# Sample rows' value and output projections as fp32 products in four column tiles, and VectorE left out of the branch around the exact path

## The chip, the cores and the metric

The kernel runs on one core of a Trainium2 chip. The metric is the device time of one execution in microseconds (us). Three runs of the kernel before took 1475.44, 1479.99 and 1482.45 us, median 1479.99. One more execution was profiled: 1477.82 us, of which the span from the first to the last instruction is 1476.1 us, with a mean granted TensorE clock of 0.99. Engines go by their short names in the profile's lines: PE is TensorE's products (PEld its weight loads), DVE is VectorE, ACT ScalarE, POOL GpSimd, SP SyncE, which issues all DMAs here. A q behind the name (DVEq) is an engine's sequencer.

## What is computed

One layer of a streaming encoder in fp32, for 1024 new rows of a prompt and 32 next rows of a running stream (the sample rows), with a model width of 1024:

```python
u = rmsnorm(x, pre_norm_g) @ w_in           # split into gq, gk, gv, gr, gg, dq, dk, dv, dg, ma, mb
...
o_gla, state = gla(gq, gk, gv, log_a)       # chunked gated linear attention with a decay
o_diff = diff_attend(rope(dq), rope(dk), dv, mask, lam)
...
yg = rmsnorm(o_gla, gla_norm_g) * silu(gg)
yd = rmsnorm(o_diff, diff_subln_g) * (1.0 - lambda_init) * silu(dg)
merged = sigmoid(ma) * (yg @ w_proj_gla) + sigmoid(mb) * (yd @ w_proj_diff)
y = x + rmsnorm(merged @ w_out, post_norm_g)
```

Three pieces matter here: the value projections (gv and dv, 1024 columns each), the last projection `merged @ w_out`, and inside the linear attention the matrix of a chunk, which weighs query t and key s by the exponential of a difference of summed decays.

## The kernel before, in words

**Products in two parts.** A matrix is split into a high part in fp32r and the rest (the low part, also fp32r), and a product becomes three: high by high, low by high, high by low. `X` holds the high and low parts of the normalized input (1024 prompt rows, then 32 sample rows), `wh` and `wl` those of weights; ScalarE makes the high part from the raw weights `wr`, VectorE or GpSimd subtracts it for the low part.

**Stages, in order.** (1) Norm and value projections, 0 to 220 us: for u = 0 to 3 a piece of 512 columns of gv and dv. A row tile has 128 rows, NQ = 8 tiles for the prompt; for each, 24 products of 512 columns run into one of two PSUM banks (`value_mm`, L295 to 308), ScalarE copies the bank to `vo`, SP stores it (`value_tile`, L283 to 293). (2) The GLA stage, 220 to about 510 us, and the attention stage after it, both with projections in between. (3) The two output branches, then `merged @ w_out` from 1372 us to the end: for u = 0 to 3 a piece of 256 columns of w_out, for each the 8 row tiles and then the sample rows (L1207 to 1238).

**The sample rows.** They fill a quarter of a row tile. In stages 1 and 3 they are the ninth tile of each u (i = NQ). `sample_pair` (L254) copies the high and low parts of the 32 rows side by side, 64 columns, into one tile `xsm` (of X) or `mgs` (of the merged rows `mg`); both use the tag "pair" with one buffer. `sample_mm` (L261) makes 16 products of it: 8 of the 64 columns with wh and 8 of the 32 high columns with wl. The result lies in PSUM rows 0 to 31 and 32 to 63; ScalarE copies one half (L291, L1223) and VectorE adds the other (L292, L1224).

**The order of the work.** In u = 0 (and for the work ahead of u = 1) the order on PE, ACT, DVE and POOL is the order of the source (`manual_schedule`). For u = 1 to 3 and in the last stage a scheduler orders each engine's queue when the kernel is built, by the source's order and by what is ready. In the GLA and attention stages PE's order alone is written by hand, by a planner (`Order`) with costs and due times; the other queues are the scheduler's. An engine takes its queue strictly in order.

**Weights of the value stage.** `wr` has one buffer, `wh` and `wl` have two; the weights of u + 1 are loaded and split while u runs. In the last stage the raw w_out pieces go through one buffer with the tag "cwr" (L1187), and the split weights of all four u stay in SBUF.

**The branch.** The fast form of a GLA head's chunk matrix (`ar`) divides the decays into two factors; where the summed decay b falls under a limit, `gla_exact` (L596) makes `ar` in an exact way instead, level by level. `gla_prep` sets a flag `fl` of one number (L554); `gla_exact` has every engine load it (L599, TENSOR_LOAD) and branch around the body (L600, COMPARE_BRANCH). With these inputs no head needs the body. In the body VectorE reads b, q and k and writes `ar`, the temporaries `t1` and `t2` among others. After it follow, per head, ScalarE's split of `ar` (L636), VectorE's in-place change of b (L643), the decayed keys k (L646) and PE's transposes of them (L654); the gated outputs go through PE's transposes L740 and VectorE's L743. L456 is GpSimd's low part of the next projection's weights.

Of the kernel before, what the change touches and what calls it, by code (L numbers as in the profile page):

```python
# [11 lines left out]
F32 = mybir.dt.float32  # L12
# [8 lines left out]
P = 128  # L21
NP = 1024
# [104 lines left out]
def hybrid_step_kernel(ctx: ExitStack, tc: tile.TileContext, a):  # L127
# [133 lines left out]
    def sample_mm(ps, pair, wh, wl):  # L261
# [4 lines left out]
        for k in range(1, KT):  # L266
            mm(ps[0:64], pair[:, k, :], wh[:, k, :], start=False, stop=(k == KT - 1))


    def value_weights(u):  # L270
        wr = v1.tile([P, KT, 512], F32, tag="wr", name="wr")
        wh = v1.tile([P, KT, 512], F32R, tag="wh", bufs=2, name="wh")
        wl = v1.tile([P, KT, 512], F32R, tag="wl", bufs=2, name="wl")
        for k in range(0, KT, 2):
            k2 = slice(k, k + 2)
            dma(wr[:, k2], a["wv"][u, :, k2])
            yield wh, wl
            act(wh[:, k2], wr[:, k2], AF.Copy)
            yield wh, wl
            ve.tensor_tensor(wl[:, k2], wr[:, k2], wh[:, k2].bitcast(F32), op=ALU.subtract)  # L280
            yield wh, wl

    def value_tile(u, i, ps):  # L283
        t0 = i * P
        dst = (gvd if u < 2 else a["newv"])[:, (u % 2) * 512 : (u % 2) * 512 + 512]
        vo = v1.tile([P, 512], F32, tag="vo", bufs=2, name="vo")
        if i < NQ:
            act(vo, ps, AF.Copy)  # L288
            st(dst[t0 : t0 + P, :], vo)
        else:  # L290
            act(vo[0:32], ps[32:64], AF.Copy)  # L291
            ve.tensor_tensor(vo[0:32], ps[0:32], vo[0:32], op=ALU.add)  # L292
            st(dst[NP:T, :], vo[0:32])

    def value_mm(i, wh, wl, meanwhile=lambda: None):  # L295
# [54 lines left out]
    with tc.manual_schedule(engines={E.PE, E.Activation, E.DVE, E.Pool}):  # L350

        def warm(n):
            ps = obank("ps_warm")
            for _ in range(n):
                mm(ps[:, 0:P], one_h, one_h, start=True, stop=True)
        warm(10)
        norm_square(0)
        s = norm_scale(0)
        warm(9)
        w0 = value_weights(0)  # L360

# [60 lines left out]
        act(le, ls, AF.Exp)  # L422
        neglam = cst.tile([P, 1], F32, name="neglam")
        ve.tensor_tensor(neglam, le[:, 1:2], le[:, 0:1], op=ALU.subtract)
        ve.tensor_scalar(neglam, neglam, LAM_INIT, None, op0=ALU.subtract)
        coef = cst.tile([P, 1], F32, name="coef")
        ve.memset(coef, 1.0)
        for r in (32, 96):
            ve.tensor_copy(coef[r : r + 32], neglam[r : r + 32])
        wv = nxt  # L430
    for u in range(1, 4):
        nxt = list(value_weights(u + 1))[-1] if u < 3 else None
        for i in range(NQ + 1):
            value_tile(u, i, value_mm(i, *wv))
        wv = nxt
        if u == 1:
            gate_rank(wgs)
# [157 lines left out]

    def gla_exact(h):  # L596

        q, k, b, qh, ql, ar, fl = gst8[h]
        flag = nc.values_load(fl[0:1, 0:1], min_val=0, max_val=1)  # L599
        with tc.If(flag > 0):  # L600
            for li, half in enumerate(LEVELS + [0]):
                mask = gp.tile([P, P], F32, tag="sm", name="mask")
                dma(mask, a["masks"][li])
                if half:
                    blk = 2 * half
                    ncol = T if blk <= NS else NP
                    e1 = gp.tile([P, T], F32, tag="t1", name="e1")
                    e2 = gp.tile([P, T], F32, tag="t2", name="e2")
                    bv = b[:, :ncol].rearrange("p (c s) -> p c s", s=blk)
                    ref = bv[:, :, half - 1 : half].to_broadcast([P, ncol // blk, blk])  # L610
                    for dst, i0, i1, src in ((e1, bv, ref, q), (e2, ref, bv, k)):
                        dv = dst[:, :ncol].rearrange("p (c s) -> p c s", s=blk)
# [3 lines left out]
                        ve.tensor_tensor(dst[:, :ncol], dst[:, :ncol], src[:, :ncol], op=ALU.mult)  # L616
                else:
                    e1, e2, ncol = q, k, T
                for c in range(9 if ncol == T else 8):
                    w = P if c < 8 else NS  # L620
                    ps = tbank("ps_e")
                    mm(ps[0:w, 0:w], e2[:, c * P : c * P + w], e1[:, c * P : c * P + w], start=True, stop=True)
                    if li == 0 or (c == 8 and half == NS // 2):
                        ve.tensor_tensor(ar[0:w, c, 0:w], ps[0:w, 0:w], mask[0:w, 0:w], op=ALU.mult)
                    else:
                        tm = gp.tile([P, P], F32, tag="sqj", name="tm")
                        ve.tensor_tensor(tm[0:w, 0:w], ps[0:w, 0:w], mask[0:w, 0:w], op=ALU.mult)
                        ve.tensor_tensor(ar[0:w, c, 0:w], ar[0:w, c, 0:w], tm[0:w, 0:w], op=ALU.add)

    def gla_head(h):  # L630
        q, k, b, qh, ql, ar, fl = gst8[h]
# [575 lines left out]
    for u in range(4):  # L1207
        wh, wl = cw[u]
        csl = slice(u * 256, u * 256 + 256)
        for i in range(NQ + 1):  # L1210
            t0 = i * P
            w = P if i < NQ else NS
            ps = (bank, dbank)[i % 2]("ps_c")[:, 0:256]
            if i < NQ:
                for k in range(KT):
                    mm(ps, mg[k][:, 0, t0 : t0 + P], wh[:, k, :], start=(k == 0), stop=False)  # L1216
                    mm(ps, mg[k][:, 1, t0 : t0 + P], wh[:, k, :], start=False, stop=False)  # L1217
                    mm(ps, mg[k][:, 0, t0 : t0 + P], wl[:, k, :], start=False, stop=(k == KT - 1))  # L1218
                src = ps
            else:  # L1220
                sample_mm(ps, mgs, wh, wl)
                tl = op.tile([NS, 256], F32, tag="tl", name="tl")
                act(tl, ps[32:64], AF.Copy)  # L1223
                ve.tensor_tensor(tl, ps[0:32], tl, op=ALU.add)  # L1224
                src = tl
            sqj = op.tile([P, 256], F32, tag="sqj", name="sqj")
            act(sqj[0:w], src[0:w], AF.Square, accum_out=ssq[0:w, i, u : u + 1])
# [97 lines left out]
```

## Time and profile before

| | before |
|---|---|
| median of the runs shown (range) | 1479.99 us (1475.44 to 1482.45) |
| profiled execution | 1477.82 us |
| its span | 1476.1 us |
| DVE busy | 789.9 us, 54% |
| ACT busy | 600.5 us, 41% |
| POOL busy | 300.2 us, 20% |
| moved by DMA | 156.58 MB |

In the lines of a timeline the columns are the start in us from the span's start, the busy time in us, engine, line, operation, out<-in by the program's names, shape and count; in brackets stands how long the engine was idle just before and what ended that. Rows that follow each other with the same form are merged (x8). A product's time contains the depth of PE's pipeline, so products overlap in these rows, and the distance of two starts is what one costs.

### The profile page before, as it was taken

Reading aid. Unit: us, or ns where it says so; the run is one execution under the profiler, and the core shown is the slowest. Engines: PE = TensorE matmul, PEld = TensorE weight load, DVE = VectorE, ACT = ScalarE, POOL = GpSimd, SP = SyncE. Lnnn points to the kernel's source line nnn. Section 1 sums busy time; section 2 is a strip of 40 time slices with the busy share of each in tenths; the row PEclk is TensorE's granted clock in tenths of the full one; section 3 lists DMA queues with packets and bytes.
Section 4 is the critical chain, followed back from the end, with each engine's and each line's share of the span. In section 5 each row is a group of like instructions: output and inputs, shape, how many; then the busy total and the mean of one; then the engine's idle time right before and its main releaser. Section 6 shows DMA issues by size and latency. Waiting matters only on the chain.

```text
span 1476.1 us, 22367 instructions
## 1 busy us (share of the span) xinstructions
PE 1422.4 (96%) x8848; PEld 1327.5 (90%) x8848; DVE 789.9 (54%) x1464; ACT 600.5 (41%) x1262; POOL 300.2 (20%) x186
## 2 busy tenths in 40 slices
PE   8999999989999999899999999999899899999997
PEld 6787779889999899899989998998899799999997
DVE  5602005756565343576776766678665536455415
ACT  4513114535354233455555555555455432221311
POOL 1200002222223124223222222222221111122001
PEclk9999999999999999999999999999999999999999
DMA  8620111122222233313232332223222278634205
GB/s 303 211 107 31 45 50 50 54 73 73 87 64 86 71 109 110 98 54 116 68 100 69 97 90 93 75 77 90 92 69 80 96 265 306 222 132 132 101 1 193
DMA packets 66742, 156.58 MB, mean 106 GB/s; under 512 B 10008, under 2 KB 28568, under 8 KB 65600
## 3 DMA queue, kind: packets, MB, share of 16 engines
q1 hardware_dynamic: 66624, 155.01, 32.5%
q8 instruction: 74, 1.21, 0.4%
q14 instruction: 44, 0.36, 0.1%
HBM read 104.39 MB, written 40.04 MB: 98 GB/s over the span
## 4 chain that ended last, share of the span: by engine, by line
PE 51%; DVE 6%; DMA 4%; ACT 2%; issue 1%; POOL 1%; SPq 0%; DVEq 0%; POOLq 0%; ACTq 0%
PE ps_w L486 9%; PE ps_w L487 9%; PE ps_w L488 9%; PE ps_w L465 2%; PE ps_w L464 2%; PE ps_w L466 2%; PE ps_s L907 2%; PE ps_t L954 2%; PE ps_s L906 2%; PE ps_c L1216 2%; PE ps_c L1218 2%; PE ps_c L1217 2%; DMA ydr<-ydd 1%; DMA kl<-kl 1%; PE po L968 1%
## 5 line engine op out<-in xcount | busy, mean ns | idle before, releaser
L486 PE MATMUL ps_w<-X,wh 128*128 128x352 f32 x1344 | 452.5, 337 | 1.4 <-DVE vo L292 1.1
L487 PE MATMUL ps_w<-X,wl 128*128 128x352 f32 x1344 | 437.7, 326 | 0.0
L488 PE MATMUL ps_w<-X,wh 128*128 128x352 f32 x1344 | 435.7, 324 | 0.0
L456 POOL TENSOR_TENSOR wl<-wr,wh 128x1024 fp32r<-128x1024 f32 x72 | 180.5, 2507 | 656.3 <-ACT wh L454 493.1
L486 PEld LDWEIGHTS ps_w<-X,wh 128*128 128x128 f32 x1344 | 255.0, 190 | 5.5 <-issue 3.0
L487 PEld LDWEIGHTS ps_w<-X,wl 128*128 128x128 f32 x1344 | 255.4, 190 | 1.2 <-issue 1.2
L488 PEld LDWEIGHTS ps_w<-X,wh 128*128 128x128 f32 x1344 | 254.7, 190 | 0.0
L912 ACT ACTIVATE p<-ps_s,nm 128x256 f32<-128x256 f32 (+7 forms) x128 | 94.6, 741 | 58.8 <-DVE ps_s L908 30.8
L306 PE MATMUL ps_v<-wh,X 128*128 128x512 f32 x248 | 97.6, 394 | 1.2 <-DVE X L245 1.2
L305 PE MATMUL ps_v<-wh,X 128*128 128x512 f32 x248 | 98.5, 397 | 0.2 <-DVE g L343 0.2
L307 PE MATMUL ps_v<-wl,X 128*128 128x512 f32 x248 | 98.3, 396 | 0.0
L454 ACT ACTIVATE wh<-wr 128x1024 fp32r<-128x1024 f32 x72 | 75.9, 1054 | 54.6 <-PE ps_w L488 30.6
L910 DVE TENSOR_REDUCE nm<-ps_s 128x1 f32<-128x256 f32 (+7 forms) x128 | 94.8, 747 | 2.7
L292 DVE TENSOR_TENSOR vo<-ps_v,vo 32x512 f32<-32x512 f32 x4 | 2.7, 678 | 140.8 <-ACT vo L291 140.8
L908 DVE MEMSET ps_s<- 64x64 f32 x128 | 14.3, 112 | 115.9 <-PE ps_s L907 114.3
L671 POOL TENSOR_TENSOR vl<-vr,vh 128x512 fp32r<-128x512 f32 (+1 forms) x20 | 24.6, 1228 | 219.4 <-ACT vh L670 219.4
L906 PE MATMUL ps_s<-k,q 128*128 128x512 f32 (+2 forms) x192 | 68.0, 362 | 1.2 <-DMA k<-k 1.2
L907 PE MATMUL ps_s<-kl,q 128*128 128x512 f32 (+2 forms) x192 | 63.8, 348 | 3.7 <-DMA kl<-kl 3.7
L288 ACT ACTIVATE vo<-ps_v 128x512 f32<-128x512 f32 x32 | 19.1, 595 | 115.1 <-PE ps_v L307 114.7
L956 ACT ACTIVATE ah<-ps_t 128x512 fp32r<-128x512 f32 (+2 forms) x96 | 46.9, 488 | 43.5 <-PE ps_t L954 42.7
L957 DVE TENSOR_TENSOR al<-ps_t,ah 128x512 fp32r<-128x512 f32 (+2 forms) x96 | 53.2, 554 | 18.3 <-ACT ah L956 17.0
L465 PE MATMUL ps_w<-Y,wl 128*128 128x352 f32 x192 | 62.2, 324 | 0.0
(319 smaller groups left out, 2968.8 us busy)
## 6 DMA issues: line engine op xcount, KB each, us to landing
wr<-w SPq DMA_DIRECT2D x72, 512.0 KB
thd<-gate SPq DMA_DIRECT2D x16, 528.0 KB
xn<-xn SPq DMA_DIRECT2D x16, 512.0 KB
wr<-wv SPq DMA_DIRECT2D x16, 512.0 KB
newk<-rr SPq DMA_DIRECT2D x8, 528.0 KB
ygr<-ygd SPq DMA_DIRECT2D x8, 528.0 KB
tha<-thd SPq DMA_DIRECT2D x8, 528.0 KB
ydr<-ydd SPq DMA_DIRECT2D x8, 528.0 KB
```

Source lines behind the costliest of these rows:

```text
L305: mm(ps, xk[:, 0, t0 : t0 + P], wh[:, k, :], start=(k == 0), stop=False)
L306: mm(ps, xk[:, 1, t0 : t0 + P], wh[:, k, :], start=False, stop=False)
L307: mm(ps, xk[:, 0, t0 : t0 + P], wl[:, k, :], start=False, stop=(k == KT - 1))
L456: nc.gpsimd.tensor_tensor(wl, wr, wh.bitcast(F32), op=ALU.subtract)
L465: mm(ps[:, :n], wl[:, k, :], src[k][:, 0, t0 : t0 + n], start=False, stop=False)
L486: mm(ps[:, :n], wh[:, k, :], src[k][:, 0, t0 : t0 + n], start=(k == 0), stop=False)
L487: mm(ps[:, :n], wl[:, k, :], src[k][:, 0, t0 : t0 + n], start=False, stop=False)
L488: mm(ps[:, :n], wh[:, k, :], src[k][:, 1, t0 : t0 + n], start=False, stop=(k == KT - 1))
L906: mm(ps[:, n0 : n0 + n], qs[m][:, qsl], ks[m][:, n0 : n0 + n], start=True, stop=False)
L907: mm(ps[:, n0 : n0 + n], qs[m][:, qsl], kls[m][:, n0 : n0 + n], start=False, stop=True)
L910: ve.tensor_reduce(nm, ps[:, 0:w], axis=AX.X, op=ALU.max, negate=True)
L912: act(p[:, 0:w], ps[:, 0:w], AF.Exp, bias=nm, accum_out=sm[:, m : m + 1])
```

## The change

It replaces the sample rows' products for u = 1 to 3 of the value stage and for all u of the last stage; u = 0 of the value stage keeps `sample_pair` and `sample_mm`. `sample_whole` adds high and low part of the 32 rows on GpSimd to one fp32 tile (tag "pair"; `xsw`, `mgs`). `sample_tiled` makes 8 products of fp32 operands, the rows' 32 columns by the raw weights, each in one of four column tiles of PE (column 0, 32, 64 or 96) with its own 32 PSUM rows; `sample_sum` adds the four parts with one ScalarE copy and three VectorE adds. In the value stage the sample tile moves from the end of u to its beginning, and reads `wr`. In the last stage each u loads its raw piece of w_out again, into the buffer "cwr".

In `gla_exact` the flag is loaded by PE, ACT, POOL and SP and no longer by VectorE. The body's VectorE work moves to GpSimd; ScalarE first copies the products out of PSUM, in groups of up to four chunks in a bank, to a tile `tm` with a tag of its own.

```diff
+    def sample_whole(src, name):
+        t = cst.tile([P, 2, KT, NS], F32, tag="pair", name=name)[:, 0]
+        for k in range(KT):
+            nc.gpsimd.tensor_tensor(t[:, k], *(src[k][:, n, NP:T].bitcast(F32) for n in range(2)), op=ALU.add)
+        return t
+
+    def sample_tiled(ps, x, w):
+        for k in range(KT):
+            r = k % 4 * NS
+            mm(ps[r : r + NS], x[:, k, :], w[:, k, :], start=k < 4, stop=k >= 4, tile_position=(0, r))
+
+    def sample_sum(dst, ps):
+        act(dst, ps[32:64], AF.Copy)
+        for r in (0, 64, 96):
+            ve.tensor_tensor(dst, ps[r : r + NS], dst, op=ALU.add)
...
+            if u:
+                sample_sum(vo[0:32], ps)
+            else:
+                act(vo[0:32], ps[32:64], AF.Copy)
+                ve.tensor_tensor(vo[0:32], ps[0:32], vo[0:32], op=ALU.add)
...
         value_tile(0, NQ, ps)
+        xsw = sample_whole(xs, "xsw")
         wgs = gate_weights()
...
     for u in range(1, 4):
+        ps = bank("ps_v")
+        sample_tiled(ps, xsw, wrs[u])
+        value_tile(u, NQ, ps)
         nxt = list(value_weights(u + 1))[-1] if u < 3 else None
-        for i in range(NQ + 1):
+        for i in range(NQ):
             value_tile(u, i, value_mm(i, *wv))
...
-        flag = nc.values_load(fl[0:1, 0:1], min_val=0, max_val=1)
+        en = mybir.EngineType
+        pv = nc.gpsimd
+        flag = nc.values_load(fl[0:1, 0:1], engines=[en.PE, en.Activation, en.Pool, en.SP], min_val=0, max_val=1)
         with tc.If(flag > 0):
...
-                        ve.tensor_tensor(dv, i0, i1, op=ALU.subtract)
-                        ve.tensor_scalar(dst[:, :ncol], dst[:, :ncol], 0.0, None, op0=ALU.min)
+                        pv.tensor_tensor(dv, i0, i1, op=ALU.subtract)
+                        pv.tensor_scalar(dst[:, :ncol], dst[:, :ncol], 0.0, None, op0=ALU.min)
...
+                    act(tm, ps.rearrange("p (c s) -> p c s", s=P)[0:w, 0:n, 0:w], AF.Copy)
...
+                        pv.tensor_tensor(to, tm, mb, op=ALU.mult)
...
-    mgs = sample_pair(mg, "mgs")
+    mgs = sample_whole(mg, "mgs")
...
     for u in range(4):
         wh, wl = cw[u]
         csl = slice(u * 256, u * 256 + 256)
+        raw = cp.tile([P, KT, 256], F32, tag="cwr", name="raw")
+        dma(raw, a["wout"][u])
...
-                sample_mm(ps, mgs, wh, wl)
+                sample_tiled(ps, mgs, raw)
                 tl = op.tile([NS, 256], F32, tag="tl", name="tl")
-                act(tl, ps[32:64], AF.Copy)
-                ve.tensor_tensor(tl, ps[0:32], tl, op=ALU.add)
+                sample_sum(tl, ps)
```

More of the change, by code (lines that the diff above doesn't have):

```diff
@@ L267, in sample_mm @@
             mm(ps[0:64], pair[:, k, :], wh[:, k, :], start=False, stop=(k == KT - 1))
+    def sample_whole(src, name):
[11 more added lines that the diff above has]
+            ve.tensor_tensor(dst, ps[r : r + NS], dst, op=ALU.add)
+    wrs = {}
     def value_weights(u):
-        wr = v1.tile([P, KT, 512], F32, tag="wr", name="wr")
+        wr = wrs[u] = v1.tile([P, KT, 512], F32, tag="wr", name="wr")
         wh = v1.tile([P, KT, 512], F32R, tag="wh", bufs=2, name="wh")
@@ L617, in gla_exact @@
                 else:
                     e1, e2, ncol = q, k, T
-                for c in range(9 if ncol == T else 8):
-                    w = P if c < 8 else NS
+                for c0 in (0, 4, 8)[: 3 if ncol == T else 2]:
+                    n, w = (4, P) if c0 < 8 else (1, NS)
                     ps = tbank("ps_e")
-                    mm(ps[0:w, 0:w], e2[:, c * P : c * P + w], e1[:, c * P : c * P + w], start=True, stop=True)
-                    if li == 0 or (c == 8 and half == NS // 2):
-                        ve.tensor_tensor(ar[0:w, c, 0:w], ps[0:w, 0:w], mask[0:w, 0:w], op=ALU.mult)
-                    else:
-                        tm = gp.tile([P, P], F32, tag="sqj", name="tm")
-                        ve.tensor_tensor(tm[0:w, 0:w], ps[0:w, 0:w], mask[0:w, 0:w], op=ALU.mult)
-                        ve.tensor_tensor(ar[0:w, c, 0:w], ar[0:w, c, 0:w], tm[0:w, 0:w], op=ALU.add)
+                    for c in range(c0, c0 + n):
+                        o = slice((c - c0) * P, (c - c0) * P + w)
+                        mm(ps[0:w, o], e2[:, c * P : c * P + w], e1[:, c * P : c * P + w], start=True, stop=True)
+                    tm = gp.tile([P, 4, P], F32, tag="tm", name="tm")[0:w, 0:n, 0:w]
+                    act(tm, ps.rearrange("p (c s) -> p c s", s=P)[0:w, 0:n, 0:w], AF.Copy)
+                    to = ar[0:w, c0 : c0 + n, 0:w]
+                    mb = mask[0:w, 0:w].unsqueeze(1).to_broadcast([w, n, w])
+                    if li == 0 or (c0 == 8 and half == NS // 2):
+                        pv.tensor_tensor(to, tm, mb, op=ALU.mult)
+                    else:
+                        pv.tensor_tensor(tm, tm, mb, op=ALU.mult)
+                        pv.tensor_tensor(to, to, tm, op=ALU.add)
```

4 lines of the change are left out of this document (1 added, 3 removed).

## The prediction

> **What bounds the kernel now.** I read the page first (busy times, waits, the chain that ended last), then the timeline of each place that the change touches, engine by engine.
>
> ```profile
> span 1476.1 us, 22367 instructions
> PE 1422.4 (96%) x8848; PEld 1327.5 (90%) x8848; DVE 789.9 (54%) x1464; ACT 600.5 (41%) x1262; POOL 300.2 (20%) x186
> ```
>
> PE is busy in 96% of the span and takes its instructions in order, so the end moves by two things only: PE time that goes away, and PE waits that grow or shrink. VectorE is busy for half the time; what it saves counts only where PE waits behind it. The profiled execution took 1477.82 us, 1.7 us more than its span and 2.2 us under the median of the runs shown (1479.99); I sum against 1477.82 and shift the result by 2.2 us.
>
> **Term 1, the value tiles of the sample rows (u = 1 to 3).** One such tile now, in the timeline of PE:
>
> ```profile
> 64.36 0.39 PE L263 MATMUL ps_v<-wh,xsm 128*64 128x512 f32 x1
> 64.59 2.01 PE L265 MATMUL ps_v<-wl,xsm 128*32 128x512 f32 x8
> 66.44 1.77 PE L267 MATMUL ps_v<-wh,xsm 128*64 128x512 f32 x7
> 68.05 0.40 PE L305 MATMUL ps_v<-wh,X 128*128 128x512 f32 x1
> ```
>
> Durations contain the pipeline; starts tell the cost. 1 + 8 + 7 = 16 products take PE from 64.36 to 68.05: 3.69 us, 0.23 us each. The new form has 8 products of fp32 operands, 32 columns wide, in the four column tiles 0, 32, 64 and 96. The trace has such work: the sample rows' attention scores, four fp32 products of 512 columns, in the tiles (row 0, column 0), (64, 32), (0, 64), (64, 96).
>
> ```profile
> 730.02 0.32 PE L488 MATMUL ps_w<-X,wh 128*128 128x352 f32 x1
> ...
> 730.26 0.65 PE L1009 MATMUL ps_ss<-kc,smp 64*32 64x512 f32 x4
> ...
> 730.72 0.63 PE L1009 MATMUL ps_ss<-kc,smp 64*32 64x512 f32 x4
> ...
> 731.15 0.26 PE L1011 MATMUL ps_ss<-smp 64*32 64x32 f32 x8
> 731.34 0.43 PE L486 MATMUL ps_w<-X,wh 128*128 128x352 f32 x1
> ```
>
> Eight records for four products: an fp32 product runs as two passes. All four first passes start together at 730.26 and the second ones at 730.72; the next work follows at 731.15. So a pass of 512 columns takes 0.43 to 0.46 us, whether one tile is at work or four. In the new form each tile has two products, four passes: 0.46 + 3 x 0.43 = 1.75 us. Going in and out costs some 0.3 us: L488 starts at 730.02 and would be followed at 730.18 (352 columns pass in 0.16 us) but is followed at 730.26; after the last short pass comes some 0.1 us of emptying, and the first product behind it is 0.1 us longer (0.43 against 0.32). That makes 2.05 us, and 1.64 us saved per tile, **4.9 us** for three.
>
> Here the trace leaves a gap: its four tiles share each row half by twos, while in the change all four use all 128 rows. Two products that share rows and differ in column (column tiles 0 and 64) do overlap in these rows, and overlap in full; that is the nearest row and I take it. The other end is products one after the other, as where all passes are in one tile:
>
> ```profile
> 748.16 1.06 PE L1041 MATMUL po_s<-vcs,smp 128*32 128x128 f32 x8
> ```
>
> Eight passes of 128 columns in about 1 us, 0.12 us each, none overlapping. Serial passes of 512 columns would make 16 x 0.43 + 0.3 = 7.2 us a tile, 3.5 us worse than now.
>
> A rule speaks against the change. The Trainium skill, TensorE: Matmul & The Clock Gate, Part 3 (what overlaps and what doesn't) says that a weight load overlaps products in flight only when its row group differs. By it the four tiles, all on one row group, would queue, and the result would be the serial rival below. The rows above disagree with it as far as they reach: tiles sharing a row half started their passes together.
>
> **Term 2, the output tiles of the sample rows.** The same for 256 columns:
>
> ```profile
> 1394.40 0.28 PE L263 MATMUL ps_c<-cwh,mgs 128*64 128x256 f32 x1
> 1394.52 1.07 PE L265 MATMUL ps_c<-cwl,mgs 128*32 128x256 f32 x8
> 1396.25 0.28 PE L1216 MATMUL ps_c<-C,m 128*128 128x256 f32 x1
> ```
>
> 1.85 us now; four passes of half the length and 0.3 us make 1.16 us: 0.7 us saved. The tile of u = 3 is the last and has a term of its own; the other three give **2.1 us**.
>
> **Term 3, the tail.** VectorE, not PE, sets the end:
>
> ```profile
> 1468.46 1.42 DVE L1236 SCALAR_TENSOR_TENSOR ogwwl<-ogwwl,s,xn 128x512 f32<-128x512 f32 x2 [0.73 <-POOL s L182]
> 1469.79 0.40 DVE L1224 TENSOR_TENSOR tl<-ps_c,tl 32x256 f32<-32x256 f32 x1
> ```
>
> The add of the last sample tile waits in VectorE's order behind the two L1236 of tile 7. An earlier PE doesn't help it, and sample_sum makes three adds of one: 2 x 0.40 = **0.8 us lost**. Elsewhere the two more adds lie beside the next tile's 24 products, 24 x 0.11 = 2.7 us (output) or 24 x 0.23 = 5.5 us (value).
>
> **Term 4, the hand-over to the GLA stage.** The sample tile now comes ahead of the eight others, so the last bank is emptied by ScalarE alone.
>
> ```profile
> 217.34 0.60 ACT L288 ACTIVATE vo<-ps_v 128x512 f32<-128x512 f32 x1 [5.00 <-PE ps_v L307]
> ...
> 221.02 0.59 ACT L291 ACTIVATE vo<-ps_v 32x512 f32<-32x512 f32 x1 [3.09 <-PE ps_v L267]
> 221.64 0.68 DVE L292 TENSOR_TENSOR vo<-ps_v,vo 32x512 f32<-32x512 f32 x1 [47.80 <-ACT vo L291]
> 222.38 0.43 PE L486 MATMUL ps_w<-X,wh 128*128 128x352 f32 x1 [1.12 <-DVE vo L292]
> ```
>
> The copy takes 0.6 us either way and the add of 0.68 us goes: of PE's wait of 1.12 us **0.7 us go**; the copy is late next.
>
> **Term 5, new waits.** xsw takes the one buffer that xsm has, so GpSimd may write it only after the products of u = 0 have read xsm, and PE's next tile wants it at once. Nearest row for the adds:
>
> ```profile
> 62.19 1.49 POOL L258 CAST xsm<-X 128x64 fp32r<-128x64 f32 x8 [3.21 <-DVE X L245]
> ```
>
> 0.19 us each: the first is there about 0.5 us after PE's 68.05, the last four are needed later than they come, and the fourth tile starts about 1 us late: at most 1.0 us. The other end is zero, if products of tile 0 stand first. The memsets of gate_weights behind the adds on GpSimd slip 5 to 7 us and ScalarE's a2s copies with them; both have the 5.5 us of a tile and more before anyone waits.
>
> The value weights are kept until the next tile read them, so wr of u + 1 loads at the start of u instead of earlier: a whole u (8 x 5.5 + 2 = 46 us) before its use, free. The raw copy of w_out is not free. It takes the buffer of the staged weights, after the last conversion:
>
> ```profile
> 1384.89 0.33 SPq L1188 DMA_DIRECT2D cwr<-wout  x1
> ...
> 1381.06 0.39 ACT L1227 ACTIVATE sqj<-ps_c 128x256 f32<-128x256 f32 x1 [2.25 <-PE ps_c L1218]
> 1381.70 2.19 ACT L1196 ACTIVATE C<-cwr 128x512 fp32r<-128x512 f32 x4 [0.17 <-DMA cwr<-wout]
> ...
> 1389.75 2.19 ACT L1196 ACTIVATE C<-cwr 128x512 fp32r<-128x512 f32 x4
> ...
> 1390.41 2.50 DVE L1197 TENSOR_TENSOR C<-cwr,C 128x512 fp32r<-128x512 f32 x4 [0.19 <-ACT C L1196]
> ```
>
> The last conversion ends at 1392.91; a load of 1 MB takes from 1384.89 to 1389.75, 4.86 us; so raw lands at 1397.8, while PE wants it at 1394.40: a wait of 3.4 us if PE's order is that of the source. It need not be: this stage has no order written by hand, and ScalarE's rows show that it goes by what is ready (L1227 of tile 2 stands ahead of the conversion of u = 2, which the source has earlier). Then products of u = 1 go first. I take 0.7 us, with 0 and 3.4 as ends; with 0.3 us for xsw, **1.0 us lost**. The copies of u = 1 to 3 have a u of 8 x 2.7 = 22 us each for 4.86 us, and SP holds nothing urgent behind them until the stores of u = 3.
>
> **Term 6, the branch.** No instruction of its body is in the trace, so the edits inside it cost nothing directly; what counts is who passes it. Four times VectorE stands still there:
>
> ```profile
> 263.70 1.23 DVE L643 TENSOR_TENSOR b<-b 128x1024 f32<-128x1024 f32 x1 [1.13 <-DVEq L600]
> 325.22 0.18 DVE L591 TENSOR_TENSOR ar<-ps_as,causal 32x32 f32<-32x32 f32 x1 [0.36 <-PE ps_as L590]
> 328.84 1.23 DVE L643 TENSOR_TENSOR b<-b 128x1024 f32<-128x1024 f32 x1 [3.45 <-DVEq L600]
> 412.55 2.77 DVE L643 TENSOR_TENSOR b<-b 128x1024 f32<-128x1024 f32 x1 [1.00 <-DVEq L600]
> 493.41 1.23 DVE L643 TENSOR_TENSOR b<-b 128x1024 f32<-128x1024 f32 x1 [3.48 <-DVEq L600]
> ...
> 260.54 2.39 POOL L456 TENSOR_TENSOR wl<-wr,wh 128x1024 fp32r<-128x1024 f32 x1 [9.40 <-ACTq L600]
> 321.95 1.05 POOL L182 TENSOR_TENSOR ss<-ss,mhalf 128x4 f32<-128x4 f32 x1 [0.17 <-DVE ss L181]
> 411.81 2.42 POOL L456 TENSOR_TENSOR wl<-wr,wh 128x1024 fp32r<-128x1024 f32 x1 [13.46 <-ACTq L600]
> 490.20 2.38 POOL L456 TENSOR_TENSOR wl<-wr,wh 128x1024 fp32r<-128x1024 f32 x1 [13.44 <-ACTq L600]
> ...
> 269.73 0.28 PE L654 MATMUL ps_kt<-ident,k 128*32 128x128 f32 x1 [0.78 <-DVE k L646]
> 332.11 0.47 PE L740 MATMUL ps_y<-ident,o_sb 128*128 128x128 f32 x1 [2.65 <-DVE yt L743]
> 498.48 0.28 PE L654 MATMUL ps_kt<-ident,k 128*32 128x128 f32 x1 [2.49 <-DVE k L646]
> ```
>
> The stall doesn't simply go. The body now reads b and writes ar on GpSimd, so VectorE's L643 (writes b) and ScalarE's ah (reads ar) wait until GpSimd is past the branch, with its instruction ahead of it done. L643 could then start at: 262.95 (end of L456) instead of 263.70, 0.75 us sooner; 325.4 (end of its own L591; L182 ends at 323.0) instead of 328.84, 3.4 us sooner; 414.25 instead of 412.55, later, but then without L456 beside it and so in 1.23 us and not 2.77, 0.2 us worse at its end; 492.6 instead of 493.41, 0.8 us sooner. PE has a wait behind each: 0.75 of the 0.78 us go; of the 2.65 us 1.85 go, as L743 must still follow the L740 before it; 0.2 us come at the third; 0.8 of the 2.49 us go. Sum 3.2 us. The lower end is 0: VectorE's own landings behind the branch were short twice (1.0 and 1.13 us) and long twice (3.45 and 3.48 us), and a long one on GpSimd, which has more code to jump over than before, gives back what it gains. I take **3.0 us**.
>
> **Sum.** 4.9 + 2.1 - 0.8 + 0.7 - 1.0 + 3.0 = 8.9 us: 1477.8 - 8.9 = 1468.9 for an execution like the profiled one, 1471.1 beside the median of the runs; I say 1471.
>
> **The rivals.** *Waits in place of the work* (15%): xsw and raw are waited for in full (4.4 us instead of 1.0) and GpSimd lands late at the branch (0 instead of 3.0): gain 2.5 us, 1477.5. For it speaks the arithmetic of term 5; against it ScalarE's order. *VectorE stays in effect at the branch* (7%): the guard still takes it along, or what waits behind it finds the same time elsewhere; gain 5.9 us, 1474. *Two streams only* (6%): on common rows no more than two tiles overlap, as many as the rows show on one row half; a tile takes 3.44 + 0.3 us, as long as now, an output tile 2.0 us: terms 1 and 2 fall to -0.6, and all to 1.3 us, 1479. *Serial tiles* (6%), the other side: four full-height tiles take turns. Value tiles lose 3 x 3.5, output tiles (16 x 0.215 + 0.3 = 3.7 us) 3 x 1.9, the tail 1.5: 10.5 + 5.7 + 1.5 + 1.0 - 0.7 - 3.0 = 15 us slower, 1495. It decides from a value tile of about 4 us up (there the gain is gone) and is slower by the bound below from some 5.7 us. *GpSimd late at the branch* (6%), also slower: its L456 ahead of the branch waits for weights (9 to 13 us idle before it); where the new order puts one whose weights come 6 us later there, ah and b wait for that: three times some 6 us against a gain of 8.9, 1489. Against it: L456 stood at that place in three of four before.
>
> **The numbers.** 0.5% of the time, about 7.4 us, is what a measurement of this kernel can tell from no change. The forecast has 60%; its own spread (raw 0 to 3.4, xsw 0 to 1, branch 0 to 3.2 and some more by other orders of the queues) puts a sixth of that under 7.4 us: faster 50%. Same: 10 + 15 + 7 + 6 = 38%. Slower: 12%. The range goes from 1462 (no new wait, 3 us more from the freed queues, and the 3 us by which the runs differ) to 1481, which takes in the waits, the branch without gain and the two streams.
>
> **What would show it.** Right: a sample tile of 16 records with four starts within 0.1 us, 2.0 us long (1.2 at the output); no DVEq at the branch and L643 right behind L456; PE's wait at the hand-over at 0.4 us. Wrong: records of the four tiles in a row at 0.43 us; PE waiting on a raw load near 1394; ah waiting on GpSimd by several us. If the stage from 220 to 510 us moves by more than 6 us either way, the queues' order has done it, and term 6 is the wrong one.

## The result

The changed kernel takes 1467.2 us (median of 6 runs, 1465.1 to 1468.5) against 1478.4 us of the kernel before beside it (6 runs, 1475.4 to 1482.7): a ratio of 0.9924, 95% interval 0.9906 to 0.9942. That is 11.2 us less by the medians (8.6 to 13.9 by the interval), where the forecast was 8.9 us. The profiled execution took 1467.32 us, with a span 10.5 us shorter than before. The page:

```profile
span 1465.6 us, 22415 instructions
PE 1411.7 (96%) x8848; PEld 1315.1 (90%) x8848; DVE 796.5 (54%) x1478; ACT 601.3 (41%) x1262; POOL 301.8 (21%) x194
```

PE is 10.7 us less busy in a span that is 10.5 us shorter; the same 96%. But read no causes from that. The busy time of PE counts overlapping products in its own way, and the waits moved as well. The places have to be looked at one by one.

**The value tiles.** The timeline of PE at u = 2 (start, duration, engine, line, operation, tiles, shape, count):

```profile
123.48 0.32 PE L358 MATMUL ps_gr<-X,wgs 128*48 128x352 f32 x1
123.73 1.92 PE L280 MATMUL ps_v<-wr,xsw 128*32 128x512 f32 x16
125.59 0.50 PE L328 MATMUL ps_v<-wh,X 128*128 128x512 f32 x1
```

Sixteen records in one tile, from 123.73 to 125.59 us; in the trace the four first passes start 7 ns apart and each next round 0.43 to 0.45 us later. With 0.09 us more going in (the L358 before it takes 0.16 us) and 0.1 us in the slower product behind, it costs 2.05 us, as forecast. At u = 1 it's another picture:

```profile
68.12 0.85 PE L267 MATMUL ps_v<-wh,xsm 128*64 128x512 f32 x3
69.43 2.53 PE L280 MATMUL ps_v<-wr,xsw 128*32 128x512 f32 x16 [0.45 <-POOL xsw L273]
71.89 0.50 PE L328 MATMUL ps_v<-wh,X 128*128 128x512 f32 x1
...
69.13 1.71 POOL L273 TENSOR_TENSOR xsw<-X 128x32 f32<-128x32 f32 x8 [4.60 <-PE ps_v L267]
```

PE would have gone on at 68.82 and starts at 69.43, 0.6 us late; then the adds, 0.21 us each, set the pace and the tile lasts 2.46 us where the next one lasts 1.86. The new wait on xsw cost 1.2 us, not 0.3.

**The hand-over** to the GLA stage: PE's wait went from 1.12 to 0.41 us, behind the copy alone.

```profile
218.24 0.43 PE L513 MATMUL ps_w<-X,wh 128*128 128x352 f32 x1 [0.41 <-ACT vo L308]
```

**The branch.** The timeline of VectorE and GpSimd at its four passes:

```profile
256.40 2.39 POOL L483 TENSOR_TENSOR wl<-wr,wh 128x1024 fp32r<-128x1024 f32 x1 [9.40 <-ACTq L630]
258.88 1.23 DVE L678 TENSOR_TENSOR b<-b 128x1024 f32<-128x1024 f32 x1 [0.44 <-POOLq L630]
...
320.43 0.18 DVE L618 TENSOR_TENSOR ar<-ps_as,causal 32x32 f32<-32x32 f32 x1 [0.36 <-PE ps_as L617]
320.54 1.20 DVE L678 TENSOR_TENSOR b<-b 128x1024 f32<-128x1024 f32 x1
...
404.38 2.43 POOL L483 TENSOR_TENSOR wl<-wr,wh 128x1024 fp32r<-128x1024 f32 x1 [13.47 <-ACTq L630]
406.89 1.23 DVE L678 TENSOR_TENSOR b<-b 128x1024 f32<-128x1024 f32 x1 [2.77 <-POOLq L630]
...
483.06 2.38 POOL L483 TENSOR_TENSOR wl<-wr,wh 128x1024 fp32r<-128x1024 f32 x1 [13.44 <-ACTq L630]
485.52 1.22 DVE L678 TENSOR_TENSOR b<-b 128x1024 f32<-128x1024 f32 x1 [2.73 <-POOLq L630]
```

VectorE no longer waits for its own landing (DVEq) but for GpSimd's, 0.1 us behind the end of L483, and not at all in the second pass, where GpSimd had nothing to do. In the third pass it starts later after its L618 than before, but takes 1.23 us and not 2.77 without L483 beside it.

**The output tiles.** The first wait on raw, and the tile of u = 1, in the timeline of PE:

```profile
1388.60 1.07 PE L280 MATMUL ps_c<-raw,mgs 128*32 128x256 f32 x16 [0.42 <-DMA raw<-wout]
...
1408.79 0.28 PE L1255 MATMUL ps_c<-C,m 128*128 128x256 f32 x1
1408.99 1.07 PE L280 MATMUL ps_c<-raw,mgs 128*32 128x256 f32 x16
1409.99 0.39 PE L1253 MATMUL ps_c<-C,m 128*128 128x256 f32 x1
```

A tile takes 1.2 us instead of 1.85 us (0.09 us in, 1.00 us, 0.12 us in the product behind). Raw's load was issued at 1383.70 us and landed after the 4.86 us that the prediction took for it; PE had put 23 products of u = 1 ahead, and 0.42 us of waiting are left. **The tail**, in the timeline of VectorE:

```profile
1457.24 1.41 DVE L1272 SCALAR_TENSOR_TENSOR ogwwl<-ogwwl,s,xn 128x512 f32<-128x512 f32 x2 [0.89 <-DMA xn<-xn]
1458.57 1.32 DVE L285 TENSOR_TENSOR tl<-ps_c,tl 32x256 f32<-32x256 f32 x3
1461.56 1.40 DVE L1272 SCALAR_TENSOR_TENSOR ogwwl<-ogwwl,s,xn 32x512 f32<-32x512 f32 x2 [0.72 <-POOL s L182]
```

Three adds take 1.32 us where one took 0.40 us.

Where the 10.5 us came from is read by pairing the same product of both traces and subtracting its starts. At the first product of the GLA stage PE is 4.1 us ahead (222.38 against 218.24 us); behind the fourth branch, at 501.43 against 492.45, 9.0 us; at the last value of the branch-free stages that follow (1271.54 against 1262.43) 9.1; behind the output tile of u = 2 (1444.47 against 1432.97) 11.5; and the tail gives back 1.0. So the tiles brought 4.1 + 2.4 us, the stage with the branches 4.9.

### The profile page after: what moved, and what is told of

It is laid out like the page before. It is cut to its first block, busy times and chain, and to the rows that moved or that the text cites. A ratio compares the mean times of both kernels' runs of the same rounds, so it can differ in the third digit from the quotient of the medians.

```text
span 1465.6 us, 22415 instructions
## 1 busy us (share of the span) xinstructions
PE 1411.7 (96%) x8848; PEld 1315.1 (90%) x8848; DVE 796.5 (54%) x1478; ACT 601.3 (41%) x1262; POOL 301.8 (21%) x194
## 4 chain that ended last, share of the span: by engine, by line
PE 49%; DMA 6%; DVE 6%; ACT 2%; issue 1%; POOL 1%; SPq 0%; DVEq 0%; POOLq 0%; ACTq 0%
PE ps_w L513 9%; PE ps_w L514 9%; PE ps_w L515 9%; PE ps_w L492 2%; PE ps_w L491 2%; PE ps_w L493 2%; PE ps_s L942 2%; PE ps_s L941 2%; PE ps_t L989 2%; DMA kl<-kl 1%; PE ps_c L1253 1%; PE ps_c L1255 1%; DMA ydr<-ydd 1%; PE ps_c L1254 1%; PE po L1003 1%
## 5 line engine op out<-in xcount | busy, mean ns | idle before, releaser
L483 POOL TENSOR_TENSOR wl<-wr,wh 128x1024 fp32r<-128x1024 f32 x72 | 180.4, 2505 | 653.4 <-ACT wh L481 502.2
L491 PE MATMUL ps_w<-Y,wh 128*128 128x352 f32 x192 | 62.0, 323 | 0.0
```

What stands on the lines that cost most here:

```text
L483: nc.gpsimd.tensor_tensor(wl, wr, wh.bitcast(F32), op=ALU.subtract)
```

## The experiments

The theory: the gain is the sum of two parts that have nothing to do with each other, the tiles (5.9 us by the prediction's terms 1 to 5) and the branch (3.0). Rivals: the tiles don't overlap, or one part alone makes all of it. The ratios that follow are to the kernel before, run beside each.

**The tiles alone.** The changed kernel with gla_exact as it was:

```diff
-        flag = nc.values_load(fl[0:1, 0:1], engines=[en.PE, en.Activation, en.Pool, en.SP], min_val=0, max_val=1)
+        flag = nc.values_load(fl[0:1, 0:1], min_val=0, max_val=1)
...
```

> The changed kernel with the branch of the kernel before (VectorE loads the flag and passes it, its body on VectorE). Theory (the parts add up: sample tiles about 6 us, branch about 4 us): 5 to 6.5 us faster than before, near 1473 where before has 1478.4 and the changed kernel 1467.2; the trace agrees with the changed kernel up to the GLA stage (4.1 us ahead of before at its first ps_w product), has the stalls of before at the branch (1.1, 3.5, 1.0, 3.5 us on VectorE), and gains 1 to 2 us again in the last stage. Rival (the branch brought nearly all, the sample tiles are given back by waits): 0 to 2 us faster than before.

Measured: 1478.3 us (12 runs), ratio 1.0007 (0.9994 to 1.0020). Nothing is gained, and the theory in its simple form fell. The trace shows where it went. At the first product of the GLA stage (4.1 us ahead in the changed kernel) this kernel is 2.8 us ahead of the kernel before (219.55 against 222.38 us), and behind the fourth branch it is 2.6 us late (504.04 against 501.43): the stage with the branches costs PE 5.4 us more. What VectorE waited for between 255 and 500 us, first in the kernel before, then in this one (us in total, times, longest):

```profile
DVE b L643 <- DVEq L600: 9.1, 4, 3.5
```

```profile
DVE b L670 <- DVEq L627: 10.1, 3, 3.5
...
DVE b L670 <- issue: 5.2, 1, 5.2
```

L643 and L670 are the same instruction, the first behind the branch. Its four idle times were 1.13, 3.45, 1.00 and 3.48 us; with the tiles, and the branch untouched, they are 5.20, 3.17, 3.43 and 3.50: 15.3 us instead of 9.1. PE waits behind them. At the first branch, where its wait was 0.78 us in the kernel before, the timeline of PE now has:

```profile
265.80 0.32 PE L515 MATMUL ps_w<-X,wh 128*128 128x352 f32 x1
270.13 0.40 PE L681 MATMUL ps_kt<-ident,k 128*32 128x128 f32 x1 [4.01 <-DVE k L673]
```

The tiles gave with one hand and the branch took it back with the other. Part of that is the clock: from 268.2 us on, still inside this wait, the granted TensorE clock is 0.5 for 6.8 us. In the kernel before, the tiles alone and the two kernels with idle work below, ten of the thirteen PE waits of 2.1 to 4.0 us in this stage have such a stretch of 3.4 or 6.8 us that starts in them or up to 1.3 us behind. In the changed kernel and the branch alone, whose waits there are at most 1.8 us, there is none; two kernels further down have one behind waits of 0.8 to 1.4 us, so the length of the wait isn't all.

**The branch alone.** The kernel before with the new gla_exact (the change's part of the diff from `flag` to the end of the function).

> The kernel before with the new branch alone; sample rows as before. Theory: 3 to 5 us faster than before (1473.5 to 1475.5): no stall of VectorE's queue at the branch, its change of b right behind GpSimd's low part of the weights, the gain complete by 510 us. Rival (the order of the queues, newly made, brought it, not the branch): 0 to 1.5 us, or a loss, and the differences spread over the stages.

Measured: 1472.3 us (12 runs), ratio 0.9965 (0.9953 to 0.9978), 5.2 us by the ratio. So it is worth 5 us beside the old tiles, but (1.0007 - 0.9924) x 1478 = 12 us beside the new ones (9 to 15 by the intervals). The two parts don't add up: 0 and 5 make 11. With VectorE out of the branch its idle times there are the same beside both: 0.44 us, none, 2.75 and 2.73 us here, 0.44, none, 2.77 and 2.73 us in the changed kernel.

**Why the idle time grew: the place of the jump.** The tiles add six VectorE instructions and two waits of its sequencer ahead of the first branch, and touch nothing near it. If the place of the jump in VectorE's stream is what matters, any other instructions will do. The kernel before with idle work in VectorE's stream (eight memsets in the value stage, then sixteen):

```diff
             ve.tensor_tensor(vo[0:32], ps[0:32], vo[0:32], op=ALU.add)
             st(dst[NP:T, :], vo[0:32])
+            pad = cst.tile([P, 2], F32, tag="pad", name="pad")
+            for _ in range((0, 2, 3, 3)[u]):
+                ve.memset(pad, 1.0)
```

> The kernel before, with eight memsets of 128x2 added to VectorE's stream in the value stage (2, 3 and 3 behind the sample tiles of groups 1 to 3), as many instructions as the tiles of the change add there, and nothing else changed. Theory: what VectorE idles at the branch depends on where in its stream the jump stands, so the four idle times move from 1.1, 3.5, 1.0, 3.5 us to those of the kernel with the tiles alone, near 5.2, 3.2, 3.4, 3.5 (6 us more), and the time is 3 to 7 us over the kernel before, although no work on the critical path was added. Rival: the place plays no part and the stalls of the kernel with the tiles alone came from its changed times; then the four stay within 0.3 us of 1.1, 3.5, 1.0, 3.5 and the time within 1 us of the kernel before.

> The same with sixteen memsets. Theory: a third place, and a third set of four idle times, each between 1.0 and 5.2 us, that differs from both sets seen by over 1 us in at least one; which, the theory can't say. Rival (place plays no part): 1.1, 3.5, 1.0, 3.5 again, within 0.3.

Measured with eight: 1485.8 us (9 runs), ratio 1.0044 (1.0030 to 1.0057), 6.5 us slower for eight memsets of two columns. What VectorE waited for at the branch, 255 to 505 us:

```profile
DVE b L646 <- DVEq L603: 10.2, 3, 3.5
DVE b L646 <- issue: 5.2, 1, 5.2
```

5.16, 3.21, 3.48 and 3.48 us: those of the tiles alone to 0.05 us, and 6.3 us more than before. PE loses 5.8 us in the stage with the branches, most of the 6.5. With sixteen, a single run of 1484.6 us:

```profile
DVE b L646 <- DVEq L603: 14.9, 4, 4.8
```

4.84, 3.11, 3.50, 3.50: neither the third pattern that the theory asked for nor the rival's old one. What falls is the thought that every place has a pattern of its own; it is rather that the kernel before stood in a place with two short landings of four, and both places tried beside it have none. No run brought the short landings back in another place, so it is not shown that the place decides, and not merely that instructions were added.

What a long landing waits for is to be seen in the view of the DMA queues at the third pass. First the kernel before, in its idle time of 1.00 us (411.55 to 412.55):

```profile
q1 hardware_dynamic: 94, 0.40, 96.5%
```

Then the same kernel in the 1.75 us behind it (412.55 to 414.30), when VectorE is at work again:

```profile
q1 hardware_dynamic: 50, 0.14, 21.2%
q8 instruction: 1, 0.02, 3.4%
q14 instruction: 1, 0.01, 1.7%
```

And the tiles alone, in the idle time of 3.43 us (412.17 to 415.60):

```profile
q1 hardware_dynamic: 144, 0.54, 40.3%
q8 instruction: 1, 0.02, 1.6%
q14 instruction: 1, 0.01, 0.8%
```

Queue q14 carries instructions, here in packets of 8 KB. In the tiles alone such a packet starts at 413.71 us, 1.2 us behind VectorE's compare-and-branch (412.52), and VectorE goes on at 415.60, 1.9 us behind the packet's start. So it is in all fourteen long idle times of the four kernels (3.1 to 5.2 us): VectorE goes on 1.8 to 1.9 us behind the start of such a packet. In the two short ones a packet follows the branch as well, at the third pass with the same 1.2 us (413.08 behind 411.89), but VectorE has gone on before it (412.55). So a packet follows the jump either way, and what differs is whether VectorE waits for it. The Trainium skill, Runtime: NRT & Kernel Launch, section Instruction fetch mechanics, states that an engine loads its instructions in sequence and that a taken branch whose target isn't among those loaded has to fetch them first. The traces agree, at 2.1 us and more for a landing; the packets on q14 are of 8 KB here where that section has blocks of 16 KiB. That VectorE's next instructions were there in the two short landings and not in the others fits this, but no view shows what an engine has loaded. Where the first pass is long it is the longest, with its packet 2.4 to 3.0 us behind the branch and not 1.0 to 1.3 as in the other three; why it comes so late, and which engine a packet of q14 belongs to, the records don't tell.

**One column.** The changed kernel with all eight products of a sample tile in one column tile:

```diff
-            r = k % 4 * NS
-            mm(ps[r : r + NS], x[:, k, :], w[:, k, :], start=k < 4, stop=k >= 4, tile_position=(0, r))
+            r = 0
+            mm(ps[r : r + NS], x[:, k, :], w[:, k, :], start=k == 0, stop=k == KT - 1, tile_position=(0, r))
...
-        act(dst, ps[32:64], AF.Copy)
-        for r in (0, 64, 96):
-            ve.tensor_tensor(dst, ps[r : r + NS], dst, op=ALU.add)
+        act(dst, ps[0:32], AF.Copy)
```

> The changed kernel with all 8 fp32 products of a sample tile in column tile 0, summed in PSUM, and so one ScalarE copy and no adds behind it. Theory (the four column tiles overlap in full, and that is the whole gain): value tiles of 16 x 0.43 + 0.3 = 7.2 us instead of 2.1, output tiles of 3.7 instead of 1.2; 3 x 5.1 + 3 x 2.5 = 23 us slower than the changed kernel, about 2 us of it back by the missing adds: 1487 to 1491, slower than before. Rival (fewer products and fp32 operands bring the gain, column tiles little): within 4 us of the changed kernel.

Measured: 1488.3 us (4 runs), ratio 1.0074 (1.0052 to 1.0097). The timeline of PE at u = 1:

```profile
69.97 7.05 PE L280 MATMUL ps_v<-wr,xsw 128*32 128x512 f32 x16 [0.45 <-POOL xsw L273]
76.96 0.50 PE L326 MATMUL ps_v<-wh,X 128*128 128x512 f32 x1
```

Sixteen passes at 0.43 us, 6.99 us in all, against 1.86 us at u = 2 in four columns. The serial rival's 7.2 us was a fair price for a case that doesn't occur: the four columns overlap in full.

**No branch at all.** The changed kernel without the call of gla_exact, so without the exact path and its guard (no instruction of its body was in any trace):

```diff
-            gla_exact(h)
```

> The changed kernel with the call of gla_exact left out: flag load, branch and the exact path are gone (the flag is never set with these inputs). Theory (what is left of the branch is VectorE waiting for GpSimd, 0.44, 2.77 and 2.73 us, and PE waiting behind it, some 0.3, 1.6 and 1.9 us, and 0.3 us four times for PE's own branch): 3 to 5 us faster than the changed kernel, near 1463. Rival (behind those waits PE is held by the next thing at once, the decayed keys or the banks): under 1.5 us.

Measured: 1468.5 us (6 runs), ratio 0.9940 (0.9921 to 0.9959), level with the changed kernel. It was thought that the remaining waits for GpSimd (5.9 us on VectorE) would be won. They go, and PE gains some 2 us each at the third and fourth branch, but it was 4.1 us late by 392 us in another order of the queues; behind the fourth branch it is level to 0.7 us. Its profiled span is 4.7 us longer, of which 3.7 us come between 1100 and 1185 us, where this execution was granted a clock of 0.5 for 10.2 us and the changed kernel's had none of that. So no cost of what is left of the branch could be measured; as the order of the queues changed with it, its price by itself stays open.

**A buffer of its own for xsw**, which takes the new wait away:

```diff
-        t = cst.tile([P, 2, KT, NS], F32, tag="pair", name=name)[:, 0]
+        t = cst.tile([P, 2, KT, NS], F32, tag="pair", name=name)[:, 0] if name == "mgs" else v1.tile([P, KT, NS], F32, name=name)
...
                 xsm = sample_pair(xs, "xsm")
+                xsw = sample_whole(xs, "xsw")
```

> The changed kernel, with the summed sample rows of the value projection in a buffer of their own and GpSimd's eight adds issued right behind the copies for group 0, so that they no longer wait for group 0's sample products to read the old contents. Theory: the wait ahead of group 1's sample tile (0.6 us) goes and the tile lasts 2.1 us instead of 2.5, so that the products are 0.9 to 1.0 us earlier when group 2 starts, and the end is 0 to 1 us earlier than the changed kernel's (1466.2 to 1467.2). Rival: the eight adds, now beside VectorE's work for the last tiles of group 0, hold that up; then the wait turns up there and group 2 starts at the same time or later.

```profile
67.29 1.08 PE L267 MATMUL ps_v<-wh,xsm 128*64 128x512 f32 x4
68.30 1.92 PE L280 MATMUL ps_v<-wr,xsw 128*32 128x512 f32 x16
70.16 0.50 PE L328 MATMUL ps_v<-wh,X 128*128 128x512 f32 x1
```

The wait is gone and the tile lasts 1.86 us; PE is 1.1 us ahead at 103 us and still 1.3 us at 923, as the theory has it. Behind that, in the attention stage, it loses 2.3 us, and its span is 0.9 us longer: 1468.4 us (6 runs), ratio 0.9925 (0.9910 to 0.9941), level with the changed kernel. In this run the microsecond at the start was not one at the end; the loss in the attention stage was not traced.

**The sample rows out of the tail.** Two kernels differ from the changed one in the order of the output tiles (tile 8 has the sample rows; an empty list is a load of raw), first this one:

```diff
-    for u in range(4):
+    for u, tiles in ((0, range(9)), (1, range(9)), (2, (0, 1, 2, 3, 8)), (3, ()), (2, (4, 5, 6, 7)), (3, (8, 0, 1, 2, 3, 4, 5, 6, 7))):
...
-        for i in range(NQ + 1):
+        for i in tiles:
```

> The changed kernel, with the sample rows of the output projection taken out of the tail: those of group 2 after its fourth tile, those of group 3 at the end of group 2, so that the last tile of all is one of 128 rows. Theory: the chain behind the last product has now the sample rows' copy, three adds and their square and normalisation behind the eighth tile's (last steps of VectorE end at 1458.65 and 1462.96 us), and loses 4.3 us of it less the 1.1 us of products that now lie ahead: 2.5 to 3.5 us under the changed kernel, 1464 to 1464.7. Rival: the weights' load for the sample rows of group 3, issued in the middle of group 2, comes late and PE waits at the end of group 2 for over 2 us; then nothing is gained.

Measured: 1469.6 us (6 runs), ratio 0.9931 (0.9916 to 0.9947); nothing gained, and by neither reason: the raw load was in time. The timeline of VectorE in the last group:

```profile
1451.12 0.42 DVE L1265 TENSOR_TENSOR ogb<-ps_c,gpost 128x256 f32<-128x256 f32 x1
...
1454.23 1.41 DVE L1273 SCALAR_TENSOR_TENSOR ogb<-ogb,s,xn 128x512 f32<-128x512 f32 x2 [2.43 <-DMA xn<-xn]
...
1463.56 1.41 DVE L1273 SCALAR_TENSOR_TENSOR ogwwl<-ogwwl,s,xn 128x512 f32<-128x512 f32 x2 [1.00 <-DMA xn<-xn]
```

The sample rows' finishing steps put VectorE behind at the start of the group. From there every tile's stores wait for VectorE, the next load of xn stands behind those stores in SP's queue, and VectorE waits for xn. So the sample rows went into the middle of groups 1 and 2, where a tile asks little of VectorE:

```diff
-    for u in range(4):
+    for u, tiles in ((0, range(9)), (1, (0, 1, 2, 3, 8)), (2, ()), (1, (4, 5, 6, 7)), (2, (8,)), (3, ()), (2, (0, 1, 2, 3)), (3, (8,)), (2, (4, 5, 6, 7)), (3, range(8))):
```

> The changed kernel, with the sample rows of the output projection in other places: group 0's at its end, group 1's after its fourth tile, group 2's at its start, group 3's after the fourth tile of group 2, each with its load of weights in time. In the run with group 3's sample rows at the end of group 2, VectorE fell behind by their finishing steps at the start of group 3 and never made it up, since each finished tile of group 3 takes 2.7 us or more of its chain against 2.72 us of products. Theory: in the middle of group 2, where a tile asks 0.4 us of VectorE, those steps cost nothing, VectorE goes through group 3 in step with the products as in the changed kernel, and the end comes 3 to 4 us after the last product's evacuation instead of 7.9: 2.5 to 3.5 us under the changed kernel, near 1464. Rival: the eight tiles of group 3 alone put VectorE behind, whatever stands ahead of them; then its last step stays 7 us or more behind the last products, and nothing is gained.

Its tail in the timelines of PE and VectorE:

```profile
1454.21 0.28 PE L1256 MATMUL ps_c<-C,m 128*128 128x256 f32 x1
...
1456.57 1.42 DVE L1273 SCALAR_TENSOR_TENSOR ogwwl<-ogwwl,s,xn 128x512 f32<-128x512 f32 x2 [0.73 <-POOL s L182]
```

From the last 128-row product to the end of the span it takes 7.1 us (1454.21 to 1461.35) instead of 10.9 (1454.74 to 1465.61), and no xn is waited for. Measured: 1464.9 us (6 runs), ratio 0.9918 (0.9901 to 0.9935). By the ratios that is 0.9 us under the changed kernel, with intervals that overlap, so this run alone doesn't show the gain that was forecast. With the buffer for xsw besides:

> The same, with the buffer of its own for the summed sample rows of the value projection, which had group 2 start 1.1 us earlier and ended level with the changed kernel. Theory: the 1.1 us is real at group 2 and given back in the attention stage by another order of queues, so it is not to be counted on: within 1 us of the run without it. Rival: what was lost there was chance of one build, and here it stays: 1 us less than the run without it.

1465.6 us (5 runs), ratio 0.9911 (0.9893 to 0.9928): as the theory has it, no difference from the one without. Last, the changed kernel and this order of tiles once more beside each other:

> The changed kernel itself, for a comparison on one chip with the next: 0.9924 of the kernel before, as measured, within 0.0018.

> The changed kernel with the sample rows in the middle of groups 1 and 2 once more. Theory (the tail's 3.7 us, seen in its profile, is a gain of the end as well): 2.5 to 3.5 us under the changed kernel beside it. Rival (of that profile's 4.3 us the greater part was the higher clock of that one execution): under 1.5 us.

The changed kernel: 1469.5 us (6 runs), ratio 0.9945 (0.9929 to 0.9960), within its first interval. The other order: 1466.4 us (6 runs), ratio 0.9914 (0.9898 to 0.9930). 3.1 us less by the medians, in the theory's range, though the two intervals just touch; the tail is again 7.2 us long. But in this profile the last 128-row product came 4.1 us later than in the changed kernel's (1458.20 against 1454.15). The sample rows that now lie ahead of it explain 1.2 us of that. Pairing the products of both traces, 2.7 us more arise at two places where the code is the same, between 560 and 640 us and between 1020 and 1040 us, and where this execution was granted a clock of 0.5 for 6.8 and 3.4 us, the changed kernel's for 3.4 us and not at all. So the shorter tail is a gain, and one execution's clock can hide it. It is probably the quickest order found; by the ratios the two comparisons put its gain at 0.9 and 4.6 us, so its size isn't settled.

## Why the prediction was right, and where it wasn't

**Terms 1 and 2, the tiles**: right to 0.05 us each in what a tile costs (2.05 and 1.2 us). The step from tiles that share a row half by twos to four of full height held, and the one column shows that the overlap is the whole of the saving: serial, the kernel is slower than before. The rule of the Trainium skill, TensorE: Matmul & The Clock Gate, Part 3, that was weighed in the prediction doesn't hold here: four tiles on the same 128 rows started their passes 7 ns apart, and seven more weight loads, up to 123.78 us, start while the first product, from 123.73 us, is in flight on those rows. *Serial tiles* and *Two streams only* fall by this.

**Terms 3 and 4**: 0.9 us for the two adds (0.8 forecast) and 0.71 us at the hand-over (0.7).

**Term 5**: raw 0.4 us (0.7 forecast; PE did put products of u = 1 ahead). The xsw wait was mis-sized: 1.2 us, over its upper bound of 1.0. The bound counted the lateness of the fourth tile and not that the second products of each tile wait for adds 5 to 8. *Waits in place of the work* needed both in full and got one.

**Term 6, the branch**: VectorE's starts came as worked out. Counted from the end of the instruction that held it: 0.1 us behind L483 three times, and right behind its own L618 once. *GpSimd late at the branch* didn't come about (L483 stood ready each time), nor did *VectorE stays in effect*. But the term was too small, and the way it was made failed. 3.0 us were worked out against the four stalls of the kernel before, as if they belonged to the branch. They hang on what VectorE does ahead of it: the tiles alone turn two short landings into long ones. Against the branch that the new tiles would have met, 15.3 us of idle VectorE, taking VectorE out is worth 12 us, and the tiles by themselves are worth nothing. The prediction had noted that the landings were short twice and long twice, and put the risk of a long one on GpSimd; it didn't ask whether the tiles' own instructions would move VectorE's. That its sum came out near is luck in this respect: both edits were made together, and the old stalls were the reference for both. By the profiled executions the gain is 1.6 us over the sum (10.5 against 8.9): the stage with the branches has 1.9 more than forecast (4.9 against 3.0), the output tiles 1.0 more (2.4 against 2.1 less 0.7; not traced), the value tiles 1.2 less (4.1 against 4.9 + 0.7 - 0.3, of which the xsw wait makes 0.9), and the tail 0.2 less.

Most of the 1.9 us can be placed. PE's gains at the four branches are 0.5, 2.7, -0.2 and 1.8 us, where 0.75, 1.85, -0.2 and 0.8 were worked out, so the excess is at the second and the fourth. There the kernel before was granted half the clock, behind PE's waits of 2.65 and 2.49 us:

```profile
331.80:335.20 3.40, 3.09 (x12) 3.09 (x13) 2.57 (x5) 2.72 (x4) 1.60 (x1) 0.50 0.41 159
499.10:502.50 3.40, 3.40 (x14) 3.22 (x14) 1.49 (x3) 1.06 (x2) 0.00 (x0) 0.50 0.04 10
```

The columns are the stretch, its length, the busy times of PE, PEld, DVE, ACT and POOL, the granted clock and the share and rate of DMA. The changed kernel had a clock of 1.0 throughout this stage. By estimate from the two places named for the last pair of runs, 3.4 us at half the clock cost PE 1.1 to 1.5 us. So the clock can account for the excess of 0.9 and 1.0 us, though no run takes the two apart. The prediction counted the waits alone and not this second price of a long one.

## What to carry to other kernels

A branch around a body that never runs has a price, and edits far away can change it: before costing any edit in a kernel with runtime branches, list each engine's idle time at every landing, and cost the edit with all of them long as well as with those of the trace. Narrow products that each leave three quarters of PE's columns empty are worth putting side by side, even at fp32's two passes. Where the last tile's finishing steps set the end, try the small odd tile where the finishing engine has slack, not merely earlier.

## What the runs showed of the hardware

Eight memsets of 128x2 on VectorE, ahead of a branch that is never entered, cost 6.5 us of 1479 (ratio 1.0044, 1.0030 to 1.0057). At such a branch VectorE idled 1.0 to 1.1 us where it went on ahead of the next 8 KB instruction packet, and 3.1 to 3.5 us, in the first pass up to 5.2, where it went on 1.8 to 1.9 us behind the start of one. In or just behind ten of thirteen PE waits of 2.1 to 4.0 us the granted clock fell to 0.5 for 3.4 or 6.8 us. Fp32 passes of 512 columns in four column tiles of 128 rows take 0.43 us a round, the same as one such pass alone.
